# Gated product over 8192 rows: groups of four rows a partition, packed in place in three 64 KiB slots, stored as one packet each by GpSimd

## The chip, the core and the metric

The kernel runs on one core of one Trainium2 chip. The metric is the device time of one execution in microseconds; lower is better. Three runs of the kernel before gave 933.0, 933.02 and 933.11 us, median 933.02. One more execution was recorded by the profiler; all durations below come from that one.

## The reference

```python
x = np.random.randn(8192, 8192).astype(np.float32)
a, b = np.split(x, 2, axis=-1)
return a * (1 / (1 + np.exp(-b)))
```

Each row of 8192 floats holds a value half `a` and a gate half `b` of 4096 floats each. The output row is `a` times the sigmoid of `b`. So 268.44 MB are read and 134.22 MB are written, and there is one sigmoid and one product for each output element.

## The kernel before

A tile gives each of the 128 partitions R = 2 neighbouring rows, so a partition's part of a tile is 64 KiB of input and 32 KiB of output, each contiguous in HBM. The first and the last tile have one row per partition (128 rows); between them lie 31 tiles of 256 rows. `n_tiles` is 33.

SBUF holds two input slots `x_sb0` and `x_sb1` (64 KiB a partition each) and two output slots `o_sb0` and `o_sb1` (32 KiB each); tile i uses slot i modulo 2 of both kinds.

Three engines work on a tile. SP issues its load (L46), on hardware queue q1. ACT replaces the gate half by its sigmoid in the input slot (L59). DVE multiplies into the output slot (L73). ACT issues the store (L83), on hardware queue q10. The final tile's two stores are issued by SP instead, and so go on q1.

The order is written out by hand in `trace` (L93 to L112): the tiles in sequence, and for each its work, then the load two tiles ahead, then its store. Semaphores carry the dependencies. `loaded` says that an input slot has landed; the load of tile i + 2 waits until DVE has done the products of tile i (L48 and L49), so that the slot is free. `product` counts finished DVE instructions, and the store waits for it (L84). `ready` joins two things that DVE must wait for: the first sigmoid of a tile, and the end of the store that last used the output slot (L62, L90).

A whole tile is one ACT instruction and one DVE instruction over 8192 elements a partition. The first tile is worked in pieces of 1024, 1024 and 2048 elements, the second and the last but one in four pieces of 2048, and the last in two. The first load has no wait, and `_launch_early` (L127) moves it ahead of the start-up barrier.

`close` (L114) drains three engines, lets GpSimd wait for the last ordinary store and clear the semaphores (L119 to L123), and lets SP wait for the final two stores (L124). GpSimd does nothing else in this kernel.

Of the kernel before, what the change touches and what calls it, by code (L numbers as in the profile page):

```python
# [6 lines left out]

P = 128
R = 2
SLOTS = 2  # L10


QUARTERS = [slice(k * 1024, (k + 1) * 1024) for k in range(4)]
HALVES = [slice(0, 2048), slice(2048, 4096)]


class _Program:


    def __init__(self, nc, x, out):  # L20
        self.nc = nc
        fp32 = mybir.dt.float32
        n_rows, n_cols = x.shape
        self.half = n_cols // 2
        self.n_tiles = n_rows // (P * R) + 1
        bounds = [0, *range(P, n_rows, P * R), n_rows]
        self.r = [(b - a) // P for a, b in zip(bounds, bounds[1:])]
        per = lambda t: [t[a:b].rearrange("(p r) m -> p (r m)", p=P) for a, b in zip(bounds, bounds[1:])]
        self.x, self.out = per(x), per(out)
        self.xs = [nc.alloc_sbuf_tensor(f"x_sb{s}", [P, R * n_cols], fp32).ap() for s in range(SLOTS)]  # L30
        self.os = [nc.alloc_sbuf_tensor(f"o_sb{s}", [P, R * self.half], fp32).ap() for s in range(SLOTS)]
        self.loaded = [nc.alloc_semaphore(f"loaded{s}") for s in range(SLOTS)]
        self.ready = [nc.alloc_semaphore(f"ready{s}") for s in range(SLOTS)]
        self.product = nc.alloc_semaphore("product")
        self.sigmoid = nc.alloc_semaphore("sigmoid")
        self.row = nc.alloc_semaphore("row")
        self.arrived = nc.alloc_semaphore("arrived")
        self.last = nc.alloc_semaphore("last")
        self.to_ready, self.stored = [0] * SLOTS, [0] * SLOTS
        self.products = self.sigmoids = self.lasts = 0  # L40
        self.done = {}

    def load(self, i, rows=None, landed=None):
        s, rows = i % SLOTS, rows or slice(0, self.r[i])
        part = slice(rows.start * 2 * self.half, rows.stop * 2 * self.half)
        ins = self.nc.sync.dma_start(out=self.xs[s][:, part], in_=self.x[i][:, part])  # L46
        ins.then_inc(landed or self.loaded[s], 16)
        if i >= SLOTS:  # L48
            ins._wait_ge(self.product, self.done[i - SLOTS])  # L49
        return ins  # L50

    def work(self, i, pieces):
        nc, s = self.nc, i % SLOTS
        rows = self.xs[s].rearrange("p (r h m) -> p r h m", r=R, h=2)
        packed = self.os[s].rearrange("p (r m) -> p r m", r=R)
        waits = []
        for k, (r, c) in enumerate(pieces):
            b = rows[:, r, 1, c]
            sig = nc.scalar.activation(out=b, in_=b, func=mybir.ActivationFunctionType.Sigmoid)  # L59
            if k == 0:  # L60
                sig._wait_ge(self.loaded[s], 16 * (i // SLOTS + 1))
                self.to_ready[s] += 1 + self.stored[s]  # L62
                waits.append((self.ready[s], self.to_ready[s]))
                sig.then_inc(self.ready[s], 1)
                self.stored[s] = 0
            else:
                if i == 1 and r.start == 1 and c.start == 0:
                    sig._wait_ge(self.row, 16)
                self.sigmoids += 1
                waits.append((self.sigmoid, self.sigmoids))  # L70
                sig.then_inc(self.sigmoid, 1)
        for (r, c), wait in zip(pieces, waits):
            mul = nc.vector.tensor_mul(out=packed[:, r, c], in0=rows[:, r, 0, c], in1=rows[:, r, 1, c])  # L73
            mul._wait_ge(*wait)
            mul.then_inc(self.product, 1)
            self.products += 1
        self.done[i] = self.products

    def store(self, i, lo=0, hi=None, products=None):
        s, final = i % SLOTS, i == self.n_tiles - 1  # L80
        hi = self.r[i] * self.half if hi is None else hi
        queue = self.nc.sync if final else self.nc.scalar
        ins = queue.dma_start(out=self.out[i][:, lo:hi], in_=self.os[s][:, lo:hi])  # L83
        ins._wait_ge(self.product, self.done[i] if products is None else products)  # L84
        if final:
            self.lasts += 16
            ins.then_inc(self.last, 16)
        else:
            self.stored[s] += 16
            ins.then_inc(self.ready[s], 16)  # L90
        return ins

    def trace(self):  # L93
        n, half = self.n_tiles, self.half
        one = slice(0, 1)
        whole = [(slice(0, R), slice(0, half))]
        fourths = [(slice(r, r + 1), c) for r in range(R) for c in HALVES]
        works = {0: [(one, c) for c in (QUARTERS[0], QUARTERS[1], HALVES[1])], 1: fourths,
                 n - 2: fourths, n - 1: [(one, c) for c in HALVES]}
        self.load(1, slice(0, 1))  # L100
        self.load(1, slice(1, 2), self.row)
        for i in range(n):
            self.work(i, works.get(i, whole))
            if i + SLOTS < n:
                self.load(i + SLOTS)
            if i == 0:
                self.store(0, 0, half // 4, 1)
                self.store(0, half // 4, half, 3)
            elif i < n - 1:
                self.store(i)  # L110
        for k, c in enumerate(HALVES):
            self.store(n - 1, c.start, c.stop, self.products - 1 + k)  # L112

    def close(self):  # L114
        nc, s = self.nc, (self.n_tiles - 2) % SLOTS
        for engine in (nc.scalar, nc.vector, nc.sync):
            engine.drain().then_inc(self.arrived, 1)  # L117
        nc.gpsimd.wait_ge(self.arrived, 3)
        nc.gpsimd.wait_ge(self.ready[s], self.to_ready[s] + self.stored[s])  # L119
        ids = sorted(h.num for h in (*self.loaded, *self.ready, self.product, self.sigmoid, self.row, self.arrived))  # L120
        assert ids == list(range(ids[0], ids[-1] + 1)) and self.last.num not in ids
        nc.gpsimd.sem_clear(range(ids[0], ids[-1] + 1))
        nc.gpsimd.drain()  # L123
        nc.sync.wait_ge(self.last, self.lasts).then_inc(self.last, -self.lasts)  # L124


def _launch_early(nc):  # L127
    SP = mybir.EngineType.SP
    entry, body = (b.instructions for b in nc.main_func.blocks[:2])
    load = next(i for i in body if i.engine == SP and i.opcode == "DMACopy")  # L130
    assert not load.sync_info.on_wait
    body.remove(load)
    where = next(k for k, i in enumerate(entry) if i.engine == SP and i.opcode == "Drain")
    entry.insert(where, load)


@with_exitstack
def kernel(
    ctx: ExitStack,
    tc: tile.TileContext,  # L140
    x: bass.AP,
    out: bass.AP,
):
    nc = tc.nc
    prog = _Program(nc, x, out)
    tc.info.no_tile_sem_insts.add(prog.load(0).ins.name)
    tc.close()
    tc.compile()  # L148
    _launch_early(nc)
    prog.trace()  # L150
    prog.close()
# [30 lines left out]
```

## Time and profile before

| what | value |
|---|---|
| median of 3 runs | 933.02 us (933.0 to 933.11) |
| profiled execution | 933.18 us, its span 931.9 us |
| DVE busy | 279.1 us, 42 instructions; 8.70 us for 128x8192 |
| ACT busy | 227.4 us, 43 instructions; 7.04 us for 128x8192 |
| loads, q1 | 5184 packets, 270.53 MB (with the final two stores) |
| stores, q10 | 4752 packets, 132.12 MB |
| load, from issue to landing | 42.2 us median |
| store, from issue to landing | 33.5 us median |

The profile counts as a packet every record of a DMA engine: a contiguous run moved for one partition (32 KiB or 64 KiB here), or the 4-byte write that counts up a semaphore at the end. A transfer over 128 partitions is shared by 16 DMA engines, 8 partitions each, so 8 data packets and one completion on every engine. Each of the 16 engines serves both queues. The shares of a queue are of the time that 16 engines have in the span. The time from issue to landing includes the wait behind transfers that were queued earlier. In the table of stretches a row gives the stretch, its length, the busy time of DVE, ACT and GpSimd (POOL) with the number of instructions, the granted TensorE clock (unused here), the busy share of the DMA engines and the GB/s that they moved. A row of the chain gives a start, a length and what took it.

### The profile page before, as it was taken

The page shows a single profiled execution, that of the slowest core. Times are in us where ns is not written, and L with a number is a line of the kernel's source. Part 1 is how long each engine was busy: PE and PEld are TensorE (multiplying, and loading weights), DVE is VectorE, ACT ScalarE, POOL GpSimd, SP SyncE. Part 2 cuts the span into 40 slices and gives each one's busy share as a digit, 9 for nine tenths or more (in the row PEclk, how much of TensorE's full clock was granted, in tenths as well). Part 3 has the DMA queues.
Part 4 walks back from the last instruction along what each step waited for, and adds up shares of the span by engine and source line. Part 5 has one row for each costly group of instructions (what it writes and reads, how often), then busy time and mean ns, then how long its engine had stood idle before and what let it go on. Part 6 is the DMA issues. An engine that isn't in the chain of part 4 may idle for free.

```text
span 931.9 us, 200 instructions
## 1 busy us (share of the span) xinstructions
DVE 279.1 (30%) x42; ACT 227.4 (24%) x43; POOL 0.2 (0%) x4
## 2 busy tenths in 40 slices
DVE  1312333123331233312333113332133321333233
ACT  2231133311333203332033320233202332023331
POOL 0000000000000000000000000000000000000000
DMA  9999999999999999999999999999999999999999
GB/s 408 443 410 439 436 440 428 437 433 425 435 442 446 416 439 433 428 444 430 446 412 439 442 425 444 436 444 414 428 447 441 435 421 449 416 443 432 428 428 405
DMA packets 9937, 402.67 MB, mean 432 GB/s; under 512 B 1104, under 2 KB 1104, under 8 KB 1232
## 3 DMA queue, kind: packets, MB, share of 16 engines
q1 hardware_dynamic: 5184, 270.53, 67.1%
q10 hardware_dynamic: 4752, 132.12, 32.8%
q14 instruction: 1, 0.01, 0.0%
HBM read 268.44 MB, written 134.22 MB: 432 GB/s over the span
## 4 chain that ended last, share of the span: by engine, by line
DMA 72%; DVE 15%; ACT 12%; DVEq 0%; issue 0%
DMA x_sb<-in_x_dram 72%; DVE o_sb L73 15%; ACT x_sb L59 12%; DVEq L117 0%
## 5 line engine op out<-in xcount | busy, mean ns | idle before, releaser
L73 DVE TENSOR_TENSOR o_sb<-x_sb 128x8192 f32<-128x8192 f32 (+2 forms) x42 | 279.1, 6659 | 645.8 <-ACT x_sb L59 645.8
L59 ACT ACTIVATE x_sb<-x_sb 128x8192 f32<-128x8192 f32 (+2 forms) x42 | 226.1, 5401 | 693.4 <-DMA x_sb<-in_x_dram 693.4
L59 ACT ACT_TABLE_LOAD x1 | 1.3, 1283 | 1.4 <-PEq L148 1.4
L166 POOL MEMSET const-bfloat16-1.0<- 128x1 bf16 x1 | 0.1, 102 | 0.0
L166 POOL MEMSET const-uint8-127<- 128x1 uint8 x1 | 0.1, 101 | 0.0
L166 POOL MEMSET const-float32-0.0<- 128x1 f32 x1 | 0.1, 99 | 0.2 <-issue 0.2
L166 POOL MEMSET const-float32-1.0<- 128x1 f32 x1 | 0.1, 98 | 0.0
## 6 DMA issues: line engine op xcount, KB each, us to landing
out_dram<-o_sb ACTq DMA_DIRECT2D x31, 4096.0 KB, 33.5
x_sb<-in_x_dram SPq DMA_DIRECT2D x4, 4096.0 KB, 25.7
out_dram<-o_sb SPq DMA_DIRECT2D x2, 1024.0 KB, 6.8
out_dram<-o_sb ACTq DMA_DIRECT2D x1, 1536.0 KB, 32.6
out_dram<-o_sb ACTq DMA_DIRECT2D x1, 512.0 KB, 15.5
x_sb<-in_x_dram SPq DMA_DIRECT2D x30, 42.2
```

Source lines behind the costliest of these rows:

```text
L59: sig = nc.scalar.activation(out=b, in_=b, func=mybir.ActivationFunctionType.Sigmoid)
L73: mul = nc.vector.tensor_mul(out=packed[:, r, c], in0=rows[:, r, 0, c], in1=rows[:, r, 1, c])
L166: nc = _bacc.Bacc("TRN2", target_bir_lowering=False, num_devices=1)
```

## The change

The 8192 rows are cut anew: one tile of 128 rows as before, then 14 groups of 512 rows with four rows a partition, then three tiles of 256 rows, then the last 128 rows. A group is 128 KiB of input and 64 KiB of output a partition.

There are no separate output slots. Three slots A, B and C of 64 KiB a partition take the loads, and products are written over inputs that are no longer needed. The first two rows of a group land in its home slot (A and C in turn), the other two in B. The product of the home rows is packed into the lower 32 KiB of the home slot, over `a` of its first row and the used gate of that row. Then the product of B's rows is packed into the upper 32 KiB of the home slot, over the second row. So the whole group lies contiguous in the home slot, 64 KiB a partition. B's sigmoid waits until both B has landed and the home product is done, since that product counts up B's `loaded` semaphore.

The group's store is issued by GpSimd, on the software queue, with `single_packet=True`, once B's product is done. B's next load is issued at the same point. The next load into a home slot waits until the store that read this slot has completed; it is issued by SP, one group later. Both loads of a group are 64 KiB a partition, with a stride of 128 KiB between partitions in HBM (64 KiB before); stores have a stride of 64 KiB (32 KiB before).

The three tiles of the tail are worked as two column halves of both rows (2x2048), and are stored by ACT as before, 32 KiB a partition. The last tile's two stores stay with SP. The first tile is stored in one piece instead of two. `close` also resets GpSimd's DMA queue.

```diff
+    def load(self, s, x, at=0, wait=None):
+        n = x.shape[1]
+        ins = self.nc.sync.dma_start(out=self.slots[s][:, at : at + n], in_=x)
+        ins.then_inc(self.loaded[s], 16)
+        self.loads[s] += 16
+        if wait:
+            ins._wait_ge(*wait)
+        return ins
...
+        first = self.sigmoids
         for k, (r, c) in enumerate(pieces):
+            gate = rows[:, r, 1, c]
+            sig = nc.scalar.activation(out=gate, in_=gate, func=mybir.ActivationFunctionType.Sigmoid)
             if k == 0:
+                sig._wait_ge(self.loaded[s], self.loads[s])
+            sig.then_inc(self.sigmoid, 1)
+            self.sigmoids += 1
+        for k, (r, c) in enumerate(pieces):
+            mul = nc.vector.tensor_mul(out=packed[:, r, c], in0=rows[:, r, 0, c], in1=rows[:, r, 1, c])
+            mul._wait_ge(self.sigmoid, first + k + 1)
+            if signal is None:
+                mul.then_inc(self.product, 1)
+                self.products += 1
             else:
+                mul.then_inc(self.loaded[signal], 1)
+                self.loads[signal] += 1
...
+        self.load(A, pairs[0][0])
+        self.load(B, pairs[0][1])
+        self.work(C, [(one, c) for c in (QUARTERS[0], QUARTERS[1], HALVES[1])])
+        self.store(nc.scalar, C, self.o_first)
+        home, other = A, C
+        pairs.append(self.x_tiles)
+        for g in range(GROUPS):
+            self.work(home, pair, signal=B)
+            self.load(other, pairs[g + 1][0], wait=(self.stored[other], self.stores[other]) if g else (self.drained, 16))
+            self.work(B, pair, to=home, to_at=half)
+            self.load(B, pairs[g + 1][1], wait=(self.product, self.products))
+            self.store(nc.gpsimd, home, self.o_groups[g], single_packet=True)
+            home, other = other, home
+        self.work(home, halves)
+        self.load(other, self.x_tiles[2], wait=(self.stored[other], self.stores[other]))
+        self.load(home, self.x_last, at=half, wait=(self.product, self.products))
+        self.store(nc.scalar, home, self.o_tiles[0])
+        self.work(B, halves)
+        self.store(nc.scalar, B, self.o_tiles[1])
+        self.work(other, halves)
+        self.store(nc.scalar, other, self.o_tiles[2])
+        self.work(home, [(one, c) for c in HALVES], at=half, to_at=half)
         for k, c in enumerate(HALVES):
+            self.store(nc.sync, home, self.o_last[:, c], half + c.start, self.products - 1 + k, last=True)
...
+        nc.gpsimd.dma_reset(range(ids[0], ids[-1] + 1))
```

In the changed kernel the load of the next home slot in the loop is line 117, the load of B line 119 and GpSimd's store line 120.

More of the change, by code (lines that the diff above doesn't have):

```diff
@@ L9 @@
 R = 2
-SLOTS = 2
+HALF = 4096
 QUARTERS = [slice(k * 1024, (k + 1) * 1024) for k in range(4)]
 HALVES = [slice(0, 2048), slice(2048, 4096)]
+GROUPS = 14
+A, B, C = range(3)
 class _Program:
@@ L23, in __init__ @@
         n_rows, n_cols = x.shape
[L24 to L31, printed above, removed]
@@ L32, in __init__ @@
-        self.loaded = [nc.alloc_semaphore(f"loaded{s}") for s in range(SLOTS)]
-        self.ready = [nc.alloc_semaphore(f"ready{s}") for s in range(SLOTS)]
+        assert n_cols == 2 * HALF and n_rows == 2 * P + 4 * P * GROUPS + 6 * P
+        self.slots = [nc.alloc_sbuf_tensor(f"slot{s}", [P, R * n_cols], fp32).ap() for s in range(3)]
+        self.loaded = [nc.alloc_semaphore(f"loaded{s}") for s in range(3)]
+        self.stored = [nc.alloc_semaphore(f"stored{s}") for s in range(3)]
         self.product = nc.alloc_semaphore("product")
@@ L35, in __init__ @@
         self.sigmoid = nc.alloc_semaphore("sigmoid")
-        self.row = nc.alloc_semaphore("row")
+        self.drained = nc.alloc_semaphore("drained")
         self.arrived = nc.alloc_semaphore("arrived")
         self.last = nc.alloc_semaphore("last")
[L39 to L49, printed above, removed]
-        return ins
@@ L52, in work, with rows @@
[L52 to L56, printed above, removed]
+        self.loads, self.stores = [0] * 3, [0] * 3
+        self.products = self.sigmoids = self.drains = 0
+        def rows(t, lo, r):
+            return t[lo : lo + r * P].rearrange("(p r) m -> p (r m)", p=P)
+        tail = P + 4 * P * GROUPS
+        cut = lambda t: (
+            rows(t, 0, 1),
+            [rows(t, P + 4 * P * g, 4) for g in range(GROUPS)],
+            [rows(t, tail + 2 * P * k, 2) for k in range(3)],
+            rows(t, n_rows - P, 1),
+        )
@@ L57, in work @@
         for k, (r, c) in enumerate(pieces):
-            b = rows[:, r, 1, c]
-            sig = nc.scalar.activation(out=b, in_=b, func=mybir.ActivationFunctionType.Sigmoid)
+            gate = rows[:, r, 1, c]
+            sig = nc.scalar.activation(out=gate, in_=gate, func=mybir.ActivationFunctionType.Sigmoid)
             if k == 0:
[L61 to L65, printed above, removed]
-            else:
[L67 to L86, printed above, removed]
+                sig._wait_ge(self.loaded[s], self.loads[s])
@@ L87, in store @@
+    def store(self, queue, s, out, at=0, products=None, last=False, **options):
+        n = out.shape[1]
+        ins = queue.dma_start(out=out, in_=self.slots[s][:, at : at + n], **options)
+        ins._wait_ge(self.product, self.products if products is None else products)
+        if last:
             ins.then_inc(self.last, 16)
-        else:
-            self.stored[s] += 16
-            ins.then_inc(self.ready[s], 16)
-        return ins
+        elif queue is self.nc.gpsimd:
+            ins.then_inc(self.stored[s], 16)
+            self.stores[s] += 16
+        else:
+            ins.then_inc(self.drained, 16)
+            self.drains += 16
@@ L93, in trace @@
     def trace(self):
-        n, half = self.n_tiles, self.half
+        nc = self.nc
         one = slice(0, 1)
[L96 to L110, printed above, removed]
+        pair = [(slice(0, R), slice(0, HALF))]
@@ new lines, in trace @@
+        halves = [(slice(0, R), c) for c in HALVES]
+        pairs = [(x[:, : 4 * HALF], x[:, 4 * HALF :]) for x in self.x_groups]
+        half = 2 * HALF
+        self.load(A, pairs[0][0])
[11 more added lines that the diff above has]
+            home, other = other, home
@@ L111, in trace @@
         for k, c in enumerate(HALVES):
-            self.store(n - 1, c.start, c.stop, self.products - 1 + k)
+            self.store(nc.sync, home, self.o_last[:, c], half + c.start, self.products - 1 + k, last=True)
     def close(self):
-        nc, s = self.nc, (self.n_tiles - 2) % SLOTS
+        nc = self.nc
         for engine in (nc.scalar, nc.vector, nc.sync):
@@ L118, in close @@
         nc.gpsimd.wait_ge(self.arrived, 3)
-        nc.gpsimd.wait_ge(self.ready[s], self.to_ready[s] + self.stored[s])
-        ids = sorted(h.num for h in (*self.loaded, *self.ready, self.product, self.sigmoid, self.row, self.arrived))
+        for s in (A, C):
+            nc.gpsimd.wait_ge(self.stored[s], self.stores[s])
+        nc.gpsimd.wait_ge(self.drained, self.drains)
+        ids = sorted(
+            h.num for h in (*self.loaded, *self.stored, self.drained, self.product, self.sigmoid, self.arrived)
+        )
         assert ids == list(range(ids[0], ids[-1] + 1)) and self.last.num not in ids
+        nc.gpsimd.dma_reset(range(ids[0], ids[-1] + 1))
         nc.gpsimd.sem_clear(range(ids[0], ids[-1] + 1))
         nc.gpsimd.drain()
-        nc.sync.wait_ge(self.last, self.lasts).then_inc(self.last, -self.lasts)
+        nc.sync.wait_ge(self.last, 32).then_inc(self.last, -32)
 def _launch_early(nc):
@@ L145 @@
     prog = _Program(nc, x, out)
-    tc.info.no_tile_sem_insts.add(prog.load(0).ins.name)
+    tc.info.no_tile_sem_insts.add(prog.load(C, prog.x_first).ins.name)
     tc.close()
```

8 lines of the change are left out of this document (added).

## The prediction

> **What bounds the kernel now.** I read the page first, then the chain that ended last, the waits, the stretches, and last the single records of DMA packets in the trace.
>
> ```profile
> span 931.9 us, 200 instructions
> DVE 279.1 (30%) x42; ACT 227.4 (24%) x43; POOL 0.2 (0%) x4
> ...
> DMA  9999999999999999999999999999999999999999
> ...
> q1 hardware_dynamic: 5184, 270.53, 67.1%
> q10 hardware_dynamic: 4752, 132.12, 32.8%
> ...
> HBM read 268.44 MB, written 134.22 MB: 432 GB/s over the span
> ```
>
> No compute engine is busy for a third of the span, and the DMA row is full in every slice. The two queue shares (loads on q1, stores on q10) add up to 99.9% of what 16 engines have. The chain seems to say otherwise:
>
> ```profile
> 482.12 42.20 DMA x_sb<-in_x_dram
> 524.31 0.02 issue
> 524.34 7.04 ACT x_sb L59
> 531.37 0.02 issue
> 531.40 8.70 DVE o_sb L73
> 540.10 0.02 issue
> 540.12 42.20 DMA x_sb<-in_x_dram
> ```
>
> It names ACT and DVE for 15.8 of every 58.00 us. But it follows one slot; the other slot's load and a store run beside that compute, as the stretches show:
>
> ```profile
> 0.00:10.00 10.00, 0.00 (x0) 1.28 (x1) 0.20 (x4) 1.00 0.92 367
> ...
> 524.00:582.00 58.00, 17.39 (x2) 14.06 (x2) 0.00 (x0) 1.00 1.00 434
> ...
> 915.00:932.00 17.00, 4.49 (x2) 3.71 (x2) 0.00 (x0) 1.00 0.90 387
> ```
>
> The next-to-last column is the DMA share. It is 1.00 in the steady state at 434 GB/s; only the first 10 us and the last 17 us fall below.
>
> The packet records give the prices. I took the time from one packet's start to the next one's on the same engine. A 32 KiB packet takes 1,209 ns and a 64 KiB load 2,414 ns where the queues alternate, so 32 KiB of data cost 1,205 ns and each packet a fixed 4 ns; a 64 KiB load followed by another load takes 2,417 ns; a completion takes about 6 ns. Two tiles are per engine 16 loads x 2,414 + 16 stores x 1,209 + 4 x 6 = 57.99 us, which is the chain's 58.00: the steady state is nothing but packets. All data, 768 units of 32 KiB per engine at 1,205 ns, are 925.4 us of the 931.9. What remains is 1.0 to 1.8 us to the first packets of the engines (mean 1.3), 0.7 us by which these first packets are long, 552 data packets x 4 to 5 ns = 2.2 to 2.8 us, 69 completions x 6 ns = 0.4 us, 0.65 us by which the slowest engine ends behind the mean, and 0.35 us after the last packet; that is nearly all of it. The same bytes move after the change, so **only this remainder can be won, while every gap in the queues would be lost**.
>
> **The change part by part.**
>
> *Fewer, larger packets.* A group of four rows per partition replaces two tiles: 16 loads and 8 stores of 64 KiB per engine, and 3 completions instead of 4. Loads now follow loads, 16 x 2,417 = 38.67 us. A 64 KiB store packet and a store inside a longer packet are in no row. From below: data alone, 2,410 ns each with loads still at 2,414, together 57.92 us. From above: 2,417 each, 58.03 us. I take one fixed cost for the whole packet, 38.67 + 19.28 + 0.02 = 57.97 us, between the 2,410 and the 2,414 of the nearest rows. Against 57.99 that is -0.02 us a group, **-0.25 us** for 14 groups (bounds -1.0 and +0.5). The first tile's store goes from two pieces to one, 8 x 4 ns; with the outer completions and the merged second load I count **-0.1 us**.
>
> *Do the queues stay full?* Let T be the landing of a group's second load on the slowest engine, P the end of its product. Landing to ACT is 0.38 us in the records; then 7.04 + 0.02 + 8.70 + 0.02: P = T + 16.2. The first half's sigmoid and product lie beside the second load. From T on, the load of the next group's first half runs, if it was queued: 8 x 2.417 = 19.3 us, so 3.2 us of it are left at P. At P, SP issues the next second load. Its packets come 1.0 us (first engine) to 1.8 us (16th) after issue, by the first load of the kernel, which found the queue empty. **1.4 us of load are left to spare** on the slowest engine. An engine that is ahead by more idles and only loses its lead.
>
> *The store, and the new wait.* At P GpSimd issues the group's store; behind it on that queue stand only later stores. L117 of the changed kernel makes SP wait for that store's completion before the load that reuses the slot one group later, and the second load (L119) and all later loads stand behind it on SP. In the records the two queues take strict turns, one load packet, one store packet, 3.62 us a pair. If the turn is a packet, a store of 8 descriptors that is one packet has one turn of 19.3 us. Started d us after P, it ends near P + d + 2.4 + 19.3, and its successor load can move 0.4 + 1.0 to 1.8 us later: P + d + 23.1 to 23.9. The loads already queued last until P + 3.2 + 19.3 + 19.3 = P + 41.8. So d may reach 18 us before a gap opens. Software issue is in no row; a hardware-queue store got its first packet 3.6 to 3.8 us after its issue behind loads, 1.0 us at an idle start. I take 4 us (bounds 1 and 18): cost **0**. Without that cover each us would cost 14 us in all.
>
> The Trainium skill, DMA: Bandwidth & Descriptors, section Queues, rings and completion order, states that each engine goes round the queues packet by packet and drains a whole packet first. The alternation above agrees; by this rule the forecast stands.
>
> *Compute.* ACT and DVE keep their 128x8192 instructions and their durations in place (7.04 and 8.70). ACT loses the store issues that stood between sigmoids, which were no bound: it waits 693.4 us for loads.
>
> *Both ends.* The early load and the first three pieces are the same, so the head stays. In the tail, each tile's pieces are 2x2048: about 3.6 us sigmoid and 2 x 4.4 us product, from the 2,048-element rows. From the last group's P the transfers still due are 3.2 + 19.3 + 19.3 + 9.7 + 19.3 + 9.7 + 9.7 + 9.7 + 4.8 = 104.7 us. The third of these tiles has landed by about P + 73 (the first five terms and 2 us of the next store); its own store is issued 0.4 + 3.6 + 8.8 us later, near P + 86, while the last load still alternates with the store before it. So the last load lands near P + 92.5; its first product ends 0.4 + 1.9 + 2.3 us later, and with 1.0 us to the first packet the final store can move at P + 98, while the tile store ahead of it runs to P + 100. Before, the same order of events left the final stores queued behind a store too. Cost 0 (from -0.7, if the slowest engine's lag goes, to +0.7). GpSimd's closing gains a DMA reset: before, that engine was finished at 927.5 and SP ended at 931.9, so 4.4 us hide it; its drains and clears there took 0.03 to 0.18 us.
>
> **Sum.** -0.25 - 0.1 = about -0.35 us on the profiled execution's 933.18 us (span 931.9 and 1.3 around it): 932.8. The median of the runs is 933.02, so 932.7 there. Own range 931.6 to 934.2, from the bounds above.
>
> **The rivals.**
>
> *Turns by descriptor, not by the declared packet (slower).* The change would then not do what it says. For: every turn in the trace is one descriptor long, and no record shows a longer one. Against: those were never joined into a packet. The store then ends at P + d + 38.7, and the loads at P + 41.8 have only 3.2 - d us behind it. The next load needs 1.4 to 2.2 us after the store, so with d above 1.0 to 1.8 the queues run dry; at d near 4 for the whole 1.4 to 2.2 us. After such a gap the following product meets more load still queued, so every second group is spared: 7 gaps, +10 to +15 us, **943 to 948 us**. Chance 0.14. The Trainium skill, same page, section SWDGE vs HWDGE vs iDMA, has a packet at 4,096 bytes preferably and at most 64 descriptors; this one holds 512 KiB in 8. Were it cut at the preferred size, the outcome would be this rival or worse; no run here shows it.
>
> *Slower packets.* The stride between partitions doubles, 128 KiB for loads and 64 KiB for stores, and the new queue takes its descriptors elsewhere. Nothing in the trace has that stride; loads at 32 and 64 KiB strides kept 1,209 and 2,414 ns. The longest 64 KiB record is 2,667 ns: all 224 grouped loads per engine at that would be +57 us, at a tenth of the excess +6 us: **935 to 990 us**. Chance 0.07. The Trainium skill, same page, section Latency and other measured facts, speaks against the change here: 207 GB/s at a pitch of 512 KiB where a padded pitch gave 214. It has no figure at 128 KiB; if that 3% held for everything here, it would be about +30 us as an estimate.
>
> *The 1.4 us to spare is not there.* If the second load's packets come up to 1 us too late in each group: 0 to +14 us, **935 to 947**. Chance 0.05.
>
> *More goes than I count.* Fixed costs at their lower bound (-1.0), the lag (-0.65) and part of the slow start: **931.0 us** or less. Chance 0.08.
>
> **How the numbers follow.** The forecast has 0.66. Faster by over 0.2% (1.9 us, about what a measurement of this kernel can tell from no change) needs the last rival: 0.08. Slower takes the three others: 0.14 + 0.07 + 0.05 = 0.26. Same: 0.66. The predicted time is 932.7. The range goes down to 931.0 and up to 944, which takes in most of the spare rival and the low ends of the two larger ones, and leaves out about 0.2.
>
> **What would show it.** Right: the profile after has 8 store packets of 64 KiB back to back on each engine, with no load between; stores land about 22 to 26 us after their issue; the DMA share is 1.00 at 434 GB/s in every group; groups repeat every 58.0 us. The first rival: stores land after 39 us or more, and the DMA row dips at every second group, with SP waiting for the store. The second: 64 KiB packets over 2.42 us. The third: a dip at each second load's issue. What would make the forecast wrong altogether is a software store that starts over 18 us late.

## The result and the profile after

The changed kernel takes 1042.57 us (median of 4 runs, 1040.21 to 1045.71) against 933.04 us: 1.118 times as long, with a 95% interval of 1.115 to 1.121. It is 109.5 us slower; the forecast was 932.7. In what follows lines are those of the changed kernel: L73 is the sigmoid, L79 the product, L55 the loads, L90 the stores. "Load B" is the load into slot B that is issued at the end of a group, together with the group's store; "home load" is the load into a home slot, which stands ahead of it in SP's order.

First the page of the changed kernel, the parts that were shown of before.

```profile
span 1044.4 us, 180 instructions
DVE 278.8 (27%) x39; ACT 227.0 (22%) x40; POOL 7.8 (1%) x18
...
DMA  9999799997999979999799997999989999889999
...
q1 hardware_dynamic: 5040, 270.53, 65.0%
q0 software_dynamic: 2016, 117.44, 26.9%
q10 hardware_dynamic: 576, 14.68, 3.3%
...
HBM read 268.44 MB, written 134.22 MB: 386 GB/s over the span
```

The same bytes and the same compute. The DMA row now has regular dents, and the queues' shares add up to 95.2% and not to 99.9%. Where the dents come from shows in what SP, which issues the loads, waited for (the columns are total us, times, longest):

```profile
SPq L55 <- DMA out_dram<-slot: 732.6, 15, 54.6
SPq L55 <- DVE slot L79: 239.2, 14, 25.2
```

Before, SP's loads waited for DVE alone:

```profile
SPq L46 <- DVE o_sb L73: 875.7, 31, 34.2
```

Now they wait for stores, and the stores are late. The page's list of transfers gives their median time from issue to landing:

```profile
out_dram<-slot POOLq DMA_DIRECT2D x14, 51.3
```

51.3 us, where the forecast had 22 to 26. The chain that ended last, over two groups:

```profile
528.28 8.70 DVE slot L79
536.98 0.28 issue
537.27 44.26 DMA out_dram<-slot
581.53 0.02 issue
581.55 22.42 DMA slot<-in_x_dram
603.97 0.02 issue
603.99 7.03 ACT slot L73
611.02 42.18 another core or an unknown queue
653.19 0.02 issue
653.22 7.04 ACT slot L73
```

A store's landing now starts the next load (537 to 581). The piece called an unknown queue is a stretch that the profile could not put down to one instruction; in the packet records loads of q1 and a store of q0 share the engines there. Two groups take 132 us. Four tiles, the same bytes, took 116. The stretches of the changed kernel:

```profile
389.00:521.00 132.00, 34.77 (x4) 28.12 (x4) 1.06 (x2) 1.00 0.95 381
...
476.00:514.00 38.00, 8.69 (x1) 6.48 (x1) 0.00 (x0) 1.00 0.99 367
514.00:522.00 8.00, 0.00 (x0) 0.78 (x1) 0.00 (x0) 1.00 0.22 90
```

There are two losses. From 514 to 522 the engines stand nearly empty. From 476 to 514 they are full and yet move only 367 GB/s: a packet takes longer. The packet records of two neighbouring groups (64 KiB packets; first packet and completions of all engines in us, mean length in ns):

```
             first    completions       mean
group 5 store   411.3   447.5 to 449.0   2418
        load B  416.1   449.9 to 451.4   2428
group 6 load B  470.3   514.5 to 520.8   3046
        store   472.7   513.5 to 520.9   2605
```

In odd groups both transfers are at full speed, in even groups they are not, all through the kernel. The packets' lengths added up, divided by 16 engines, give the time that a mean engine is busy; the rest of the span it is idle. (The records overlap by a few ns, so that this idle time is 1 to 3 us too small in each run.) Before: 931.8 busy and 0.1 idle. After: 994.2 and 50.2. So of 112.5 us **62.4 are longer packets and 50.1 are idle engines**. Added up by transfer, some 45 of the 62.4 us lie in the stores and loads B of the even groups. Some 18 lie in the home loads, in their first packets after a gap (3.06 us on average in group 5) and their last ones before a store (3.60 us there).

### The profile page after: what moved, and what is told of

The parts are those of the page before. It is cut to its first block, busy times and chain, and to the rows that moved or that the text cites. A ratio compares the mean times of both kernels' runs of the same rounds, so it can differ in the third digit from the quotient of the medians.

```text
span 1044.4 us, 180 instructions
## 1 busy us (share of the span) xinstructions
DVE 278.8 (27%) x39; ACT 227.0 (22%) x40; POOL 7.8 (1%) x18
## 4 chain that ended last, share of the span: by engine, by line
DMA 56%; another core or an unknown queue 27%; ACT 10%; DVE 6%; issue 0%; DVEq 0%; SPq 0%
DMA out_dram<-slot 33%; DMA slot<-in_x_dram 23%; ACT slot L73 10%; DVE slot L79 6%; DVEq L137 0%; SPq L55 0%
## 5 line engine op out<-in xcount | busy, mean ns | idle before, releaser
L79 DVE TENSOR_TENSOR slot<-slot 128x8192 f32<-128x8192 f32 (+3 forms) x39 | 278.8, 7160 | 757.4 <-ACT slot L73 757.4
L73 ACT ACTIVATE slot<-slot 128x8192 f32<-128x8192 f32 (+3 forms) x39 | 225.7, 5801 | 805.1 <-DMA slot<-in_x_dram 805.1
L90 POOL DMA_DIRECT2D out_dram<-slot x14 | 7.6, 541 | 926.7 <-DVE slot L79 926.7
## 6 DMA issues: line engine op xcount, KB each, us to landing
out_dram<-slot POOLq DMA_DIRECT2D x14, 51.3
```

The lines of the kernel that those rows point to most:

```text
L73: sig = nc.scalar.activation(out=gate, in_=gate, func=mybir.ActivationFunctionType.Sigmoid)
L90: ins = queue.dma_start(out=out, in_=self.slots[s][:, at : at + n], **options)
```

## The experiments

Each run's time is a median, beside runs of the kernel before at 933.0 us on the same chip; the interval is that of its ratio to these. Busy and idle are the two numbers just explained. The diffs are cut to the lines that matter; `group=True` only tells the helper that this store counts up the semaphore of its slot.

### One part of the change at a time

The changed kernel with its stores on ACT's hardware queue:

```diff
-            self.store(nc.gpsimd, home, self.o_groups[g], single_packet=True)
+            self.store(nc.scalar, home, self.o_groups[g], group=True)
```

> The changed kernel with its group stores on ACT's hardware queue, without the one-packet flag; slots, waits and sizes as they are. Theory T (turns by descriptor): the trace of the changed kernel has load and store packets in strict turns, so the flag does nothing, the store lands late and SP's wait for it empties the queues every second group; then the queue that issues it hardly matters: 1030 to 1045 us, the dips stay. Rival Q (the software queue stretches the packets): the 64 KiB packets return to 2,418 ns and only the gaps stay: 940 to 980 us.

Measured: 1042.94 us (1.116 to 1.120), 993.4 busy, 50.1 idle, the same long packets in the same groups. The software queue is not the cause.

The changed kernel without the flag:

```diff
-            self.store(nc.gpsimd, home, self.o_groups[g], single_packet=True)
+            self.store(nc.gpsimd, home, self.o_groups[g])
```

> The changed kernel with single_packet=True left out, still on GpSimd's software queue. Theory T: nothing changes, 1038 to 1048 us, same turns. If the flag did harm or good (rival F: it makes the packets long or holds the turn in some groups): clearly another time, below 1030 or above 1055 us.

Measured: 1041.2 us (1.114 to 1.118), the same turns, one load packet, one store packet. The flag changes nothing that the trace shows.

The kernel before with the wider strides alone:

```diff
+            for i in range(1, self.n_tiles - 2, 2):
+                both = t[bounds[i] : bounds[i + 2]].rearrange("(p k r) m -> k p (r m)", p=P, k=2)
+                parts[i], parts[i + 1] = both[0], both[1]
```

> The kernel before, with only the rows dealt out otherwise: two neighbouring tiles share groups of four rows a partition, so that loads have a stride of 128 KiB and stores of 64 KiB between partitions, as in the changed kernel; slots, queues, packet sizes and waits as before. Rival S (the wider stride stretches the packets): 64 KiB loads at 2,600 ns or more and 950 to 1030 us. Theory T and rival Q: 933 us, packets at 2,418 ns.

Measured: 932.97 us (0.999 to 1.001). A stretch of it, 434 GB/s as before:

```profile
524.00:582.00 58.00, 17.38 (x2) 14.06 (x2) 0.00 (x0) 1.00 1.00 434
```

The kernel before with its stores on the software queue:

```diff
-        queue = self.nc.sync if final else self.nc.scalar
+        queue = self.nc.sync if final else self.nc.gpsimd
...
+            nc.vector.wait_ge(self.drained[s], self.drains[s])
```

> The kernel before, with its 32 KiB-a-partition stores issued by GpSimd on the software queue (no flag) instead of ACT; DVE gets a separate wait for the earlier store. Rival Q (the software queue itself is slow): longer packets, 945 to 1000 us. Theory T: the output slots and the loads have the same slack as before, so 933 to 936 us.

Measured: 933.39 us (0.9995 to 1.0013). From 307 us on, the first store packet mostly comes 6.4 to 6.9 us after the issue, not 3.7 to 4.1 as before, and the time stays the same. After these four, the queue, the flag and the stride are cleared. What is left is the size of a store against a load in the turns, and the waits around it.

### Where the long packets sit

```diff
-A, B, C = range(3)
+C, B, A = range(3)
```

> The changed kernel with slots A and C in each other's place in SBUF (one line), all else the same. In the changed kernel, packets of load and store are long (means 3.0 and 2.6 us) in groups 0, 2, 4 and so on, which store from A, and at 2,418 ns in the odd ones, which store from C. Theory H (something in HBM or in the timing): the long packets stay with the even groups, 1035 to 1050 us. Rival B (place in SBUF): they move to the odd groups.

Measured: 1040.8 us (1.113 to 1.118). The long packets stay with the even groups: not the place of the home slot.

```diff
-            [rows(t, P + 4 * P * g, 4) for g in range(GROUPS)],
+            [rows(t, P + 4 * P * (g ^ 1), 4) for g in range(GROUPS)],
```

> The changed kernel with the groups' rows taken in the order 1, 0, 3, 2, and so on; the schedule is the same and only addresses in HBM change. Rival X (some pairs of HBM addresses collide): the long packets move to other steps or come in all, and the time changes by over 20 us. Theory H in its timing form (the even steps come without a gap before them, the odd ones just after one): long packets stay in steps 0, 2, 4 and so on, 1035 to 1050 us.

Measured: 1039.0 us (1.111 to 1.116), long packets in steps 0, 2, 4 and so on: they go with the step, not with the group's rows.

### Turns and lateness

The changed kernel with loads in two halves:

```diff
+        for k in range(0, n, 2 * HALF):
+            ins = self.nc.sync.dma_start(out=self.slots[s][:, at + k : at + k + 2 * HALF], in_=x[:, k : k + 2 * HALF])
```

> The changed kernel with every 64 KiB-a-partition load issued as two of 32 KiB a partition, so that in the strict turns the store moves 64 KiB for 32 KiB of load. Theory T (the store is late because of its share of the turns): the store ends some 29 us after its first packet, not 38, before the queued loads are done, the gaps go, at least 6 us for each two groups: 950 to 990 us if the long packets stay, 932 to 940 if they go too. Rival W (the wait is not the cause of the gaps): 1030 us or more.

Measured: 1017.0 us (1.089 to 1.093), 961.9 busy, 49.8 idle. Neither forecast fits. The packets are mostly good and the stores land in time, but now the engines run empty once in every group. Stretches around it:

```profile
386.00:392.00 6.00, 4.43 (x1) 0.00 (x0) 0.53 (x1) 1.00 0.52 186
392.00:396.00 4.00, 0.00 (x0) 1.92 (x1) 0.00 (x0) 1.00 0.94 279
```

In the records most engines end the queued load at 387.3, the product comes at 390.5, the next packets at 391.4: one engine was 6.2 us behind the others when load B landed, and the product waits for the last engine. It is the third rival in a larger form (the spare time isn't there), and the restart at 279 GB/s costs again.

The kernel before with loads in two halves (its load routine, with the same loop):

> The kernel before, with every 64 KiB load issued as two of 32 KiB, so that load and store take turns at equal size as in the changed kernel, but with its own output slots, where a store has 58 us until its slot is needed. Theory M (equal turns of loads and stores are by themselves slow in HBM): packets longer than 1,213 ns and 950 us or more. Theory T alone: 933 to 936 us, 128 x 31 more load packets at some 4 ns each per engine's share add about 1 us.

Measured: 965.0 us (1.031 to 1.038), 953.3 busy, 8.4 idle. The turns themselves are clean: from 448 to 460 us both kinds have 1,213 ns at 433 GB/s. But load and store now share equally and the load lands later, so that once in two tiles the queue is empty on nearly all engines when the product comes (at 440), and the first packets after it take 2,159 to 2,822 ns on 15 engines. Theory M falls: of the extra 32 us, 21.5 are longer packets, nearly all at these restarts, and 8.3 are idle engines.

The one-queue version of the changed kernel:

```diff
+            self.store(nc.sync, home, self.o_groups[g], group=True)
             self.load(B, pairs[g + 1][1], wait=(self.product, self.products))
-            self.store(nc.gpsimd, home, self.o_groups[g], single_packet=True)
```

> The changed kernel with the group's store issued by SP on the loads' own hardware queue, ahead of the next load into B, so that it goes whole in its place in one queue and never takes turns with a load: the one turn of 19.3 us that was forecast. Theory T (sharing by turns, with what follows from it, is the whole loss): packets at 2,418 ns, no dips, 932 to 940 us. Rival L (64 KiB stores, packing in place or the three slots cost by themselves): 960 us or more.

Measured: 942.35 us (1.008 to 1.011), 939.7 busy, 1.5 idle. The store's time to landing, and two long stretches:

```profile
out_dram<-slot SPq DMA_DIRECT2D x14, 23.4
```

```profile
60.00:408.00 348.00, 104.31 (x12) 82.04 (x13) 0.00 (x0) 1.00 1.00 434
408.00:872.00 464.00, 139.15 (x17) 111.23 (x17) 0.00 (x0) 1.00 1.00 427
```

A store of one turn lands in 23.4 us, as was forecast for the changed kernel, and 100 of that kernel's 109.5 us are gone, with the slots, the packing and the 64 KiB stores still there. Sharing the engines by turns, with what follows from it, is the loss. The last 9 us are another matter.

The same with the store behind the load:

```diff
             self.load(B, pairs[g + 1][1], wait=(self.product, self.products))
-            self.store(nc.gpsimd, home, self.o_groups[g], single_packet=True)
+            self.store(nc.sync, home, self.o_groups[g], group=True)
```

> As the one-queue version, but with the store behind the load into B: no turns either, and the store as late as it can be, so that the next load into a home slot waits until the queue is empty. It prices a late store alone. Theory T: one gap of 1.4 to 2.2 us in each group and a slow first packet (some 0.6 us), 14 times, 960 to 975 us, packets otherwise at 2,418 ns. Rival L: more than 990 us.

Measured: 985.5 us (1.055 to 1.058), 953.9 busy, 29.7 idle: 10 us above the range of theory T. Stretches of one group:

```profile
420.00:426.00 6.00, 0.00 (x0) 0.00 (x0) 0.00 (x0) 1.00 0.50 175
426.00:460.00 34.00, 8.69 (x1) 7.03 (x1) 0.00 (x0) 1.00 1.00 432
460.00:464.00 4.00, 0.00 (x0) 0.00 (x0) 0.00 (x0) 1.00 1.09 344
```

The first row is the late store's gap: the engines are idle, and the first packets after it take 2,982 ns on average (2,982 to 3,174 over the groups). The third was in no forecast: as all engines turn from load to store at once, the last load packet takes 3,583 ns on average, 1.2 us more than the others, and 3,363 to 3,602 in every group but the first. Another 5 us of idle time come in the tail (from 963 to 968).

The kernel before on one queue:

```diff
-        queue = self.nc.sync if final else self.nc.scalar
+        queue = self.nc.sync
```

and the store is issued ahead of the load.

> The kernel before with its stores on SP, ahead of the load issued at the same point, so that one queue carries everything and there are no turns. At each product 19.3 us of load or more are queued, so no gap: 932 to 935 us. If turns cost the kernel before anything, it shows here as a gain; if a single queue costs something, as a loss.

Measured: 938.9 us (1.005 to 1.009), above the range. From 292 to 872 us it runs at 434 GB/s as before, so turns cost the kernel before nothing there; the 5.9 us are lost in the first 292 us (427 GB/s, before 432) and in the tail (386 GB/s in its last 37 us, 410 in the last 32 of before).

### The order of the first packets

The changed kernel with B's work over half the columns:

```diff
-            self.work(B, pair, to=home, to_at=half)
+            self.work(B, [(slice(0, R), HALVES[0])], to=home, to_at=half)
```

> The changed kernel with its turns and its software queue, but B's sigmoid and product taken over the first half of the columns only; half of the upper rows' outputs are therefore not computed. The group's product then comes some 8 us sooner after the landing, so that 11 us of load instead of 3 are left when store and next load are issued. If the long packets of the even groups come from the queue running short at that moment (theory N: engines then start store and load in different order and stay out of step): all groups look like the odd ones, 932 to 960 us. If the turns stretch packets whatever the start (theory M): 1000 us or more.

Measured: 949.6 us (1.016 to 1.020), 942.7 busy, 4.5 idle. The time is in the range of theory N. In no group are the store or load B long (2,418 to 2,474 ns on average), and in all of them the store's first packet comes 6.0 to 14.5 us ahead of load B's.

B's work in two halves, with nothing left out (`halves` in place of `pair`):

> The changed kernel with B's work in each group cut into two column halves of both rows, nothing left out: the second sigmoid runs beside the first product, so that the group's product comes some 12.7 us after the landing instead of 16.2 and 6.7 us of load are left then, not 3.2. Theory N (the long packets come where the queue runs short as store and load are issued): packets at 2,418 ns in all groups but for the first ones, what remains are late stores by up to 1 or 2 us a group and the turn from loads to stores: 945 to 970 us. Theory M (sharing by turns stretches packets in every second group whatever is left): 1000 us or more.

Measured: 978.9 us (1.041 to 1.054), 957.8 busy, 18.1 idle, between the two forecasts. One group in fourteen has long packets, and it is the only one whose load came first (by 1.2 us).

The store held back:

```diff
+            nc.gpsimd.wait_ge(self.product, self.products)
+            for _ in range(3):
+                nc.gpsimd.memset(self.scratch, 0.0)
+                nc.gpsimd.drain()
```

> The changed kernel with GpSimd's store held back by three fills of a scratch tile (some 3 us) after the product, so that load B's packets are first on all engines. Theory N: the queue is as short as before when the load comes, so the even groups keep their long packets, and later stores cost about 3 us more in a group: 1060 to 1090 us. Rival O (what matters is that some engines begin with the store and others with the load): long packets gone, 990 to 1030 us.

Measured: 1091.6 us (1.168 to 1.172), 1011.4 busy, 80.3 idle. Groups 2 to 13 are all long (2,499 to 2,603 ns for stores, 2,923 to 3,036 for loads), and in all of them the load came first, with 5.3 to 5.4 us of load still queued at the product. So a short queue is not it, and theory N falls, though the time lay near its forecast. Rival O as it was put here, with the long packets gone, falls too.

The one-queue version with B in halves:

> The one-queue version with B's work in two halves. If the one-queue version's 9 us over the kernel before come from the short queue at the product, they go: 933 to 936 us. If they come from the turn between 19 us of stores and 19 us of loads on all engines at once: 939 to 944 us, no better.

Measured: 937.4 us (1.003 to 1.006), 937.0 busy, 0.6 idle, between the two forecasts: some 5 of the 9 us are gone. The packets show that this is not simply half of one loss. In the one-queue version 7.9 us are longer packets: 4.6 in the stores, nearly all in the last packet of each, and 2.7 in the loads B, mostly in the first. With B in halves these are gone, and 5.0 us come in the home loads instead, in the last packet ahead of each store (2,528 to 3,050 ns on average, from the second group on).

Load B held back instead of the store:

```diff
-            self.load(B, pairs[g + 1][1], wait=(self.product, self.products))
             self.store(nc.gpsimd, home, self.o_groups[g], single_packet=True)
+            for k in range(3):
+                nc.gpsimd.memset(self.scratch[:, 1024 * k : 1024 * (k + 1)], 0.0).then_inc(self.held, 1)
+            self.load(B, pairs[g + 1][1], wait=(self.held, 3 * (g + 1)))
```

> The changed kernel with load B held back instead of the store: SP waits until GpSimd has issued the store and then filled three pieces of a scratch tile (some 3 to 4 us). Nothing is left out. The queue is as short at that moment as in the changed kernel or shorter. Theory O (after the run with the later store, where the load led in every group and packets were long in every group: they are long where a group's load leads the turns, and not where its store leads): packets at 2,418 ns in all groups but for the first one or two of each turn from loads to stores, 960 to 1000 us. Theory N (the short queue makes them long): long packets in the even groups at least, 1040 us or more.

Measured: 974.2 us (1.040 to 1.048), 959.7 busy, 11.7 idle. Load B's packets are at 2,417 to 2,427 ns in all 14 groups. Its DMA row and the store's time to landing:

```profile
DMA  9999999999999999999999999999999999999999
```

```profile
out_dram<-slot POOLq DMA_DIRECT2D x14, 43.1
```

Making each load wait 3 us more makes the kernel 68 us faster. What remains long is mostly the first packet of a store (3.7 us on average in groups 5 and 6), at the turn from loads to stores.

Five fills in place of three before the store:

> The run with the held-back store, with five fills in place of three, so that the store's first packet comes two packets of load B after it (some 4.8 us or more) and not one. In all traces so far, a group has long packets exactly where its load leads its store by one packet (2.4 to 3.4 us), and the one group where the load led by two (the first of the run with the held-back store, 4.8 us) was at 2,417 and 2,508 ns. Theory I (the same packet index of load and store next to each other, as when the load leads by one, makes them long): packets near 2,420 ns in most groups though the load leads; the later store costs idle time, 1030 to 1080 us. Theory O (a leading load makes them long): all groups long, 1110 us or more.

Measured: 1014.2 and 1033.2 us in two executions; the trace is that of the 1033.2 us. One of the two lies in the range of theory I and one below it, both far below that of theory O. From group 2 on the groups alternate, and it is the distance that decides. Lead of the first store packet over load B's first (us), and mean lengths (ns):

```
group   lead of store   store   load B
  4         -5.9         2418     2559
  5         -2.8         2594     2972
  6         -5.8         2417     2548
  7         -2.7         2569     2943
```

A load that leads by two packets leaves the store's packets at 2,417 ns; its own mean of 2,550 holds the turn from loads to stores. A load that leads by one makes both long. The one group of the run with three fills whose load led by two packets, its first (4.8 us), agrees: 2,418 ns for the store and 2,508 for load B.

One small fill before the load:

> The run with the held-back load, with one fill of 16 columns in place of three of 1,024, so that load B is issued some 2.5 us sooner and many engines should begin with one store packet, then the load. Theory O: the store still leads, packets at 2,420 ns, 960 to 980 us. Theory I says nothing on a store that leads by one; if the distance of one packet in either direction makes them long, the groups with a lead of some 2.4 us show 2.6 and 3.0 us packets, 1000 us or more.

Measured: 985.4 us (1.050 to 1.062), 5 us above the range of theory O. The store leads by 2.4 to 2.7 us in eight groups and by 4.8 in six. Stores are at 2,417 to 2,436 ns and loads at 2,417 to 2,510 in all of them: a store that leads by one packet does not make them long.

## Why the prediction was wrong

**Right:** the DMA engines bound the kernel, compute is hidden, nothing but the small remainder could be won and every gap is lost. A clean 64 KiB packet costs what was taken (2,418 ns long in the records; the 2,414 to 2,417 of the prediction are from start to start). The stride and the software queue cost nothing in themselves. The first store packet's delay (6.1 us after issue in group 5) lay within the bounds of 1 to 18 us, but "cost 0" for it held only with the one turn: with shared turns, holding the store back by some 3.5 us more cost 49 us.

**The step that failed** is in the part on the store and the new wait: "If the turn is a packet, a store of 8 descriptors that is one packet has one turn of 19.3 us." It has eight turns. With the flag and without it, where both queues have packets ready, the engines go over to the load after every 64 KiB descriptor. The rule of the Trainium skill, DMA: Bandwidth & Descriptors, section Queues, rings and completion order, that an engine drains a whole packet before it changes queues, was read together with the flag; either the flag made no packet of 8 descriptors here or the engine does not hold its turn for one. The trace does not tell which, and the time is the same. So the rival with a chance of 0.14 was the true mechanism: stores land in 51.3 us, SP waits 732.6 us for them, the dents come in every second group, as that rival had it.

**Its price was wrong** by seven to eleven times, 10 to 15 us where 109.5 were measured. Three terms were missing or too small.

- The gap was put at 1.4 to 2.2 us, from a store that ends on all engines at once. In the seven long gaps the mean engine is idle for 5.3 to 5.9 us each, 39 us in all; the rest of the 50.1 us are short breaks in other places. In group 6 the first engine was done with load and store by 515 us and the last at 520.9, the next load is issued only after the last, and its first packet comes at 522.4.
- Packets were held at their price whatever the order. In the even groups they are 0.6 us (loads B) and 0.2 us (stores) longer, some 45 us in all. The engines lose step in such groups: in group 6 of the run with the held-back store the first packets of load B start within 0.6 us of each other and the last ones within 5 us.
- The home loads were taken as clean. Their packets right after a gap and right before a store are longer, some 18 us in all.

**Why the even groups are long** could be narrowed to one condition. In every group-store trace looked at for it (the changed kernel, and the runs with the hardware queue, without the flag, with slots or groups swapped, with B in half and in halves, and with load or store held back), a group has a long store and a long load B just where load B's first packet comes ahead of the store's by one packet, 1.2 to 3.5 us. It has not where the load leads by 4.8 us or more, nor where the store leads. In the changed kernel the thin spare time is what brings the two so close. In the even groups some 3 us of load are left at the product (2.7 to 4.1 on the mean engine), and load B's packets come first; in the odd ones, after a gap, 6.7 to 7.0 us are left, and the store comes first by two packets. With more spare time (B in half and in halves) the store came first in 27 of 28 groups.

What makes them long under this condition stays open. When the load leads by one, load and store packets with the same place in their transfers follow each other on each engine; but they do so too where the store leads by one, and there they are clean, so this alone is not the cause. Moving the home slots in SBUF or the groups' rows in HBM changed nothing. With 32 KiB packets on both sides (the kernel before with loads in halves) the load also came first, and the packets in the turns were clean, which points to size as a part of it; that kernel differs in other ways too.

**Even with the turn held,** the forecast would have been short. The one-queue version is that case, and takes 942.35 us and not 932.7: "cost 0" left out that packets get longer where a queue goes over from one kind of transfer to the other (5.2 us in the one-queue version with halves, 7.9 in the one without). The spare time of 1.4 us was too thin as well, since cutting B's work in halves takes 5 us of the 9 away.

No version of the changed kernel here beats the kernel before. The nearest is the one-queue version with halves, 4.4 us above it.

## What to carry to other kernels

A flag or a rule that a change rests on should be priced as not working until a trace shows it: here the forecast put the wait at 0 because of a turn of eight packets that no row showed, and the wait came onto the critical path. Where a load has to wait for a store, work out when the store ends on the slowest engine with its real share of the turns, and leave spare time for several packets, not for one. When engines are full and the rate is low, look at the lengths of single packets and at which queue began: 3 us more or less at the start of a group were worth 50 to 70 us.

## What the runs showed of the hardware that was not expected

- Two queues that share the engines changed turns after each packet of 32 or 64 KiB, on the hardware queues (the kernel before, the run on ACT's queue) and on the software queue, with `single_packet` (the changed kernel) or without (the run without the flag).
- 64 KiB loads and stores in equal turns ran at 2,418 ns a packet, but for packets at a turn, when the store led (the run with load B held back, the odd groups of the changed kernel) or when the load led by two packets or more (the run with five fills); they took about 3.0 and 2.6 us on average when the load led by one. The cause is open.
- Packets next to a change from one kind of transfer to the other can be long, and how long differs: the last load packet ahead of the store took 3,363 to 3,602 ns on average with the store last on one queue, 2,528 to 3,050 in the one-queue version with halves, and 2,418 to 2,505 in the one-queue version, where the last store packet took up to 3,004. The first packets after an empty queue took 2,982 to 3,174 ns with the store last.
- With loads queued ahead, the group's first store packet came 6.1 us after its issue from the software queue and 6.3 us from the hardware queue (group 5). The 32 KiB stores of the kernel before got theirs after 3.7 to 4.1 us from the hardware queue, and from the software queue after 3.7 to 4.1 us at first and mostly 6.4 to 6.9 later. What share of this is the queue's and what the packets ahead of it, no run separated.
